# Split weights of the MLPs and the convolution in buffers of 2,112 instead of 2,048 bytes, so that they start at all multiples of 64 modulo 512

## The chip, the cores and the metric

The kernel runs on one NeuronCore of one Trainium2 chip. The metric is the device time of one execution in microseconds. Most executions of one program agree within 0.3%.

## The reference

Two layers of a trunk on x of 512 tokens by 1,024 channels, float32. Layer 0 mixes with sparse attention, layer 1 with a convolution; behind each mixer stands an MLP with squared ReLU. Cut to what matters here:

```python
h = x
for i in range(2):
    hn = rmsnorm(h, norm_mix_g[i])
    y = dsa_mixer(hn, ...) if i == 0 else conv_mixer(hn, ...)
    h = h + y
    h = h + sq_relu_mlp(rmsnorm(h, norm_mlp_g[i]), mlp_w1[i], mlp_w2[i])
return rmsnorm(h, final_g)

def sq_relu_mlp(h, w1, w2):              # w1 1024 x 4096, w2 4096 x 1024
    return jnp.square(jax.nn.relu(h @ w1)) @ w2

def conv_mixer(h, w_pw1, b_pw1, w_dw, b_dw, ln_g, ln_b, w_pw2, b_pw2):
    a = h @ w_pw1 + b_pw1                # 1024 x 2048
    u = a[..., :1024] * jax.nn.sigmoid(a[..., 1024:])
    u = causal_depthwise_conv(u, w_dw) + b_dw          # 31 taps a channel
    u = jax.nn.silu(layernorm(u, ln_g, ln_b))
    return u @ w_pw2 + b_pw2             # 1024 x 1024
```

## The kernel before

**Products in three parts.** Each float32 operand of a product is split into a high part, rounded to fp32r by ScalarE, and a low part, the difference, which VectorE (or GpSimd) makes. `split` (L80) does this for the weights: a loaded block `wraw` of 512 columns a partition becomes the tiles `whi` and `wlo`, 2,048 bytes a partition each. `mm3` (L90) then issues three fp32r matmuls, high by high (L91), high by low (L92), low by high (L93). Activations lie channel by token in tiles of 512 tokens: `hT` is the residual, `ghi`/`glo` the split normed input, `hh`/`hl` the split hidden activations of an MLP.

**Who is moving and who is stationary.** In the up-projections, in the down-projection of layer 0 and in both products of the convolution mixer the weights are stationary: 128 columns, 512 bytes a partition, a quarter of a `whi` or `wlo` tile, while 512 tokens (2,048 bytes), or 256 where the mixer works in halves, move past them. In the down-projection of layer 1 it is the other way round: 128 tokens of `hh`/`hl` are stationary and a whole `whi` or `wlo` tile of 512 columns moves; its banks are `dps`.

**Stages.** Attention of layer 0 (0 to about 275 us of the span), MLP of layer 0 (to about 640 us), convolution mixer (to about 842 us), MLP of layer 1 (to the end). An MLP is worked in four groups of 1,024 hidden channels: eight blocks up, eight blocks (layer 0) or two halves of four banks (layer 1) down, each of 8 x 3 matmuls of 512 columns a block. That makes 1,536 matmuls of 512 columns in the MLP of layer 0. In the MLP of layer 1 it is 1,488, since the first two up blocks are done in halves inside the convolution stage.

**Where the tiles lie.** A pool lays its buffers one behind the other. The pool `wsplit_att` holds five buffers each of `whi` and `wlo` for the attention; `wsplit_mid` (the second entry of the list `wsplit`) holds twelve of each from there on. `whole` rounds such tiles up to multiples of 512 bytes, and a tile `fill` of 64 bytes stands ahead of the others. In the built program all operands of fp32r matmuls start at a multiple of 512 bytes: `ghi` at 38,400 + 2,048 c, the `whi` buffers of `wsplit_mid` at 97,792 + 2,048 k, its `wlo` buffers at 122,368 + 2,048 k, with k = 0 to 11 in turn.

**The depthwise convolution.** For each of eight channel blocks c, `taps` (L753) shares 31 taps between engines. TensorE takes the first in plain float32 matmuls of 32-row diagonals `diag` by shifted copies `sh4` (L780), four of them side by side in the array. ScalarE makes products `pt` from the shifted tile `u` (L788; the first of a block goes into `pa`, L786), and GpSimd adds them into `pa` (L790). VectorE does the rest of the taps (L798 or L802), reading `u` at steps of 4 bytes. `u` tiles are 2,168 bytes long. `pt` has four buffers, so ScalarE can be four products ahead of GpSimd.

The order of instructions on an engine comes from the framework's scheduler, except where `manual_schedule` fixes it.

Of the kernel before, what the change touches and what calls it, by code (L numbers as in the profile page):

```python
# [9 lines left out]
F32 = mybir.dt.float32  # L10
F32R = mybir.dt.float32r
# [7 lines left out]
P = 128  # L19
S = 512  # L20
# [23 lines left out]
ROW = 512  # L44
FILL = 64


@with_exitstack
def kernel(
# [17 lines left out]
    def whole(n):  # L67

        return -(-4 * n // ROW) * ROW // 4
# [9 lines left out]
    wsplit = []  # L79

    def split(src, eng=None, pool=None, tag="w", bufs=None):

        a, b = src.shape[1], src.shape[2]
        hi, lo = ((pool or wsplit[-1]).tile([P, whole(a * b)], F32R, tag=tag + x, name=tag + x, bufs=bufs)
                  [:, :a * b].rearrange("p (a b) -> p a b", a=a) for x in ("hi", "lo"))
        nc.scalar.activation(hi, src, AF.Copy)  # L86
        (eng or nc.vector).tensor_sub(lo, src, hi.bitcast(F32))  # L87
        return hi, lo
# [14 lines left out]
    def proj(w, x2, eng=None, off=0):  # L103
# [7 lines left out]
        def unit(j, kh):  # L111
            i = (j + off) // 2
            j0, j1 = max(2 * i - off, 0), min(2 * i - off + 2, KC)
            if i not in raws:
                if len(raws) > 1:
                    raws.pop(next(iter(raws)))
                raws[i] = load(w, 0, KC, j0 * P, (j1 - j0) * P)
            return split(raws[i][:, kh * 4:kh * 4 + 4, (j - j0) * P:(j - j0 + 1) * P], eng)
# [46 lines left out]
    def vec(name, c=0):  # L165
        if name == "mix":
            return pm0[:, c:c + 1]
        return pv[:, vecs[name] + c:vecs[name] + c + 1]
# [51 lines left out]
    with tc.tile_pool(name="wsplit_att", bufs=5) as ws, \  # L220
# [39 lines left out]
        def v_parts(half, kb):  # L260


            ws = {}
            for k, b in kb:
                if k not in ws:
                    if k == 0:
                        vps.clear()
                    if k // 4 not in v_raw:
                        v_raw.clear()
                        v_raw[k // 4] = load(w_in, k // 4 * 4, 4, 2 * D + half * S, S)  # L270
                    ws[k] = split(v_raw[k // 4][:, k % 4:k % 4 + 1, :], nc.vector if half == 0 and k < 3 else nc.gpsimd)
                    if k == KC - 1:
                        v_raw.clear()
                if b not in vps:
                    vps[b] = bank(f"vps{b}")
                hi, lo = ws[k]
                tb = slice(b * P, (b + 1) * P)
                mm3(vps[b], ghi[k][:, tb], glo[k][:, tb], hi[:, 0, :], lo[:, 0, :], k == 0, k == KC - 1)
                yield
# [5 lines left out]
        with tc.tile_pool(name="setup", bufs=1) as setup:  # L285
# [13 lines left out]
            for i in range(4):  # L299
                xs.append(setup.tile([P, NB, 2 * P], F32, name=f"xs{i}"))  # L300
                nc.sync.dma_start(xs[i], xv[:, :, i * 2 * P:(i + 1) * 2 * P])
                t = setup.tile([P, whole(2 * nx)], F32, name=f"xw{i}")
# [4 lines left out]
            n = 0  # L307
# [20 lines left out]
            def stream(k):  # L328
                hi, lo = split(xw[k // 2][:, k % 2:k % 2 + 1, 2 * P:], nc.gpsimd, setup, "xw", 2)
                hi, lo = hi[:, 0, :], lo[:, 0, :]  # L330
                first, last = k == 0, k == KC - 1
                mm3(k_ps[:nkw], hi[:, 2 * P:], lo[:, 2 * P:], ghi[k], glo[k], first, last)
                for j in range(2):
                    js = slice(j * P, (j + 1) * P)
                    mm3(q_ps[j][:, P:], hi[:, js], lo[:, js], ghi[k][:, P:], glo[k][:, P:], first, last)
# [397 lines left out]
    with tc.tile_pool(name="cv", bufs=1) as cv, \  # L733
# [7 lines left out]
        with tc.tile_pool(name="cv_t", bufs=2) as cv_t:  # L741
# [14 lines left out]
            def taps(c, cs, npe, npool):  # L756

                u, v = us[c], vs[c][:, cs]
                n = cs.stop - cs.start
                p0 = 4 * npe  # L760
                d0 = p0 + npool

                def sh(t, more=0):
                    return u[:, cs.start + t:cs.stop + t + more]

                def wt(t):
                    return cw[:, c, t:t + 1]


                w = n + 4 * (npe - 1)  # L770
                flat = dram.tile([P, w + 3], F32, name=f"flat{c}_{cs.start}")
                nc.sync.dma_start(flat, sh(0, w + 3 - n))
                sh4 = cv_t.tile([P, 4, S + 4 * (TAPS // 4 - 1)], F32, tag="sh4", name="sh4")
                for z in range(4):
                    nc.sync.dma_start(sh4[z * 32:(z + 1) * 32, :, :w],
                                      flat.rearrange("(j i) x -> i j x", j=4)[:, :, z:z + w])
                cps = cv_ps.tile([P, S], F32, tag="conv", name="conv")[:, :n]
                for a in range(npe):
                    for j in range(4):
                        nc.tensor.matmul(cps[j * 32:(j + 1) * 32, :], diags[c][:, a, j, :], sh4[:, j, 4 * a:4 * a + n],  # L780
                                         start=a == 0, stop=a == npe - 1)
                pa = cv_t.tile([P, S], F32, tag="pa", name="pa", bufs=5)[:, :n]
                for t in range(p0, d0):
                    pt = pa if t == p0 else cv_t.tile([P, S], F32, tag="pt", name="pt", bufs=4)[:, :n]
                    if t == p0:
                        nc.scalar.activation(pt, sh(t), AF.Identity, bias=vec("bdw", c), scale=wt(t))  # L786
                    else:
                        nc.scalar.activation(pt, sh(t), AF.Copy, scale=wt(t))  # L788
                    if t > p0:
                        nc.gpsimd.tensor_add(pa, pa, pt)  # L790
                if c:
                    if npool:
                        nc.gpsimd.tensor_add(pa, pa, pilot[:, cs])
                    else:
                        nc.scalar.activation(pa, pilot[:, cs], AF.Identity, bias=vec("bdw", c))
                if c in ASIDE:
                    for t in range(d0, TAPS):
                        nc.vector.scalar_tensor_tensor(pa, sh(t), wt(t), pa, op0=OP.mult, op1=OP.add)  # L798
                    nc.vector.tensor_add(v, cps, pa)
                else:  # L800
                    for t in range(d0, TAPS - 1):
                        nc.vector.scalar_tensor_tensor(cps, sh(t), wt(t), cps, op0=OP.mult, op1=OP.add)  # L802
                    nc.vector.tensor_add(cps, cps, pa)
                    nc.vector.scalar_tensor_tensor(v, sh(TAPS - 1), wt(TAPS - 1), cps, op0=OP.mult, op1=OP.add)
# [60 lines left out]
            def first(c):  # L865
                cs = slice(0, S) if c < WHOLE else halves[0]
                taps(c, cs, *TAPS0[c])
                stat(c, cs)
# [21 lines left out]
            def second(c):  # L890
                taps(c, halves[1], *TAPS1[c])
                stat(c, halves[1])
# [146 lines left out]
```

## Time and profile before

| | |
|---|---|
| median of 3 runs | 1187.91 us (1186.22 to 1188.4) |
| the profiled execution's own time | 1186.75 us |
| its span, first to last instruction | 1185.0 us |
| mean granted TensorE clock | 0.989 |
| PE busy | 1150.8 us, 97% of the span |
| DVE busy | 663.3 us, 56% |
| ACT busy | 498.2 us, 42% |
| POOL busy | 247.5 us, 21% |

PE is TensorE's matmuls, PEld its loads of stationary operands, DVE VectorE, ACT ScalarE, POOL GpSimd. Matmuls overlap in the pipeline: one of 512 columns shows as 389 ns long, while the next starts long before. Its cost in a row of matmuls is the distance from one start to the next.

### The profile page before, as it was taken

To read this page: it belongs to the slowest core of one execution; us is meant where nothing else is said; L and a number is where in the kernel's file an instruction comes from. 1 tells how busy PE (TensorE), PEld (TensorE's weight loads), DVE (VectorE), ACT (ScalarE), POOL (GpSimd) and SP (SyncE) were. 2 spreads that over 40 slices of the span, in tenths; PEclk is the share of its full clock that TensorE was granted. 3 is DMA by queue.
4 is the path that set the end of the run, shared out by engine and by line. 5 is a ranking of instruction groups with operands and counts; after the bars stand their busy time and mean duration, and the time that the engine had idled before them with its cause. 6 is when DMAs were issued, how large, how long until landed. Compare 5 with 4: busy or idle time off the path is not lost.

```text
span 1185.0 us, 15284 instructions
## 1 busy us (share of the span) xinstructions
PE 1150.8 (97%) x5828; PEld 948.5 (80%) x5828; DVE 663.3 (56%) x1195; ACT 498.2 (42%) x936; POOL 247.5 (21%) x248
## 2 busy tenths in 40 slices
PE   7999999999999999999999988899999999999997
PEld 6778888877888888888888666689888888888886
DVE  4589854476434434434444998878544434434434
ACT  5353454545423423423435544466632432432422
POOL 2436643322005000000012667632100000000000
PEclk8999999999999999999999998999999999999999
DMA  6122222215233323322323563533322332332211
GB/s 229 36 71 72 89 84 77 71 36 182 78 100 107 98 80 107 107 83 78 125 71 116 151 172 91 161 108 115 117 86 92 107 107 72 106 107 92 86 36 71
DMA packets 104353, 117.84 MB, mean 99 GB/s; under 512 B 3817, under 2 KB 87609, under 8 KB 104280
## 3 DMA queue, kind: packets, MB, share of 16 engines
q1 hardware_dynamic: 102440, 112.89, 30.6%
q10 hardware_dynamic: 1840, 3.97, 0.9%
q8 instruction: 46, 0.75, 0.3%
q14 instruction: 27, 0.22, 0.1%
HBM read 112.56 MB, written 4.29 MB: 99 GB/s over the span
## 4 chain that ended last, share of the span: by engine, by line
PE 81%; DVE 12%; DMA 2%; issue 2%; ACT 1%; POOL 1%; SPq 0%; POOLq 0%; DVEq 0%; ACTq 0%
PE mm L91 19%; PE mm L93 19%; PE mm L92 19%; PE dps L93 5%; PE dps L92 5%; PE dps L91 5%; DVE score L482 2%; DVE m L480 2%; DVE conv L802 2%; DVE wlo L87 2%; DVE pa L798 1%; PE vps L91 1%; PE vps L92 1%; PE vps L93 1%; DMA xs<-in_x_dram 1%
## 5 line engine op out<-in xcount | busy, mean ns | idle before, releaser
L86 ACT ACTIVATE whi<-wraw 128x512 fp32r<-128x512 f32 x378 | 234.6, 631 | 469.9 <-PE mm L92 317.1
L92 PE MATMUL mm<-glo,whi 128*128 128x512 f32 (+1 forms) x928 | 337.0, 365 | 1.2 <-DVE glo L175 1.2
L93 PE MATMUL mm<-ghi,wlo 128*128 128x512 f32 (+1 forms) x928 | 337.1, 365 | 0.0
L91 PE MATMUL mm<-ghi,whi 128*128 128x512 f32 (+1 forms) x928 | 334.6, 366 | 1.9 <-ACT whi L86 0.8
L87 DVE TENSOR_TENSOR wlo<-wraw,whi 128x512 fp32r<-128x512 f32 x325 | 233.5, 726 | 177.7 <-ACT whi L86 174.1
L92 PEld LDWEIGHTS mm<-glo,whi 128*128 128x128 f32 x928 | 175.0, 189 | 31.0 <-issue 2.4
L91 PEld LDWEIGHTS mm<-ghi,whi 128*128 128x128 f32 x928 | 173.1, 189 | 32.6 <-issue 2.8
L93 PEld LDWEIGHTS mm<-ghi,wlo 128*128 128x128 f32 x928 | 175.0, 189 | 28.7 <-issue 1.1
L93 PE MATMUL mm<-hh,wlo 128*128 128x512 f32 x256 | 99.6, 389 | 0.0
L92 PE MATMUL mm<-hl,whi 128*128 128x512 f32 x256 | 99.6, 389 | 0.0
L92 PE MATMUL dps<-wlo,hh 128*128 128x512 f32 x256 | 99.6, 389 | 0.0
L91 PE MATMUL mm<-hh,whi 128*128 128x512 f32 x256 | 99.1, 389 | 0.0
L91 PE MATMUL dps<-whi,hh 128*128 128x512 f32 x256 | 99.1, 389 | 0.0
L93 PE MATMUL dps<-whi,hl 128*128 128x512 f32 x256 | 98.6, 389 | 0.0
L636 DVE SCALAR_TENSOR_TENSOR hr<-mm,rmsb 128x512 f32<-128x512 f32 x64 | 44.1, 691 | 91.9 <-PE mm L93 90.2
L87 POOL TENSOR_TENSOR wlo<-wraw,whi 128x512 fp32r<-128x512 f32 x53 | 70.9, 1342 | 89.6 <-ACT whi L86 89.5
L183 POOL TENSOR_TENSOR fr<-v,mhalf 128x1 f32<-128x1 f32 x4 | 2.2, 548 | 340.2 <-DVE v L181 340.2
L642 DVE TENSOR_TENSOR hl<-hf,hh 128x512 fp32r<-128x512 f32 x64 | 44.6, 697 | 41.9 <-ACT hh L641 41.9
L206 POOL TENSOR_TENSOR ss<-sq 128x512 f32<-128x512 f32 (+1 forms) x4 | 5.7, 1434 | 270.3 <-ACT sq L201 270.3
L790 POOL TENSOR_TENSOR pa<-pa,pt 128x512 f32<-128x512 f32 (+1 forms) x43 | 53.6, 1249 | 32.6 <-ACT pt L788 30.5
L92 PEld LDWEIGHTS mm<-hl,whi 128*128 128x128 f32 x256 | 48.0, 188 | 10.1
L92 PEld LDWEIGHTS dps<-wlo,hh 128*128 128x128 f32 x256 | 48.0, 188 | 10.0
(257 smaller groups left out, 1588.2 us busy)
## 6 DMA issues: line engine op xcount, KB each, us to landing
wraw<-in_mlp_w_dram SPq DMA_DIRECT2D x64, 1024.0 KB, 5.2
wraw<-in_conv_w_pw_dram SPq DMA_DIRECT2D x12, 1024.0 KB
wraw<-in_dsa_w_in_dram SPq DMA_DIRECT2D x10, 1024.0 KB, 9.1
wraw<-in_dsa_w_out_dram SPq DMA_DIRECT2D x4, 1024.0 KB, 4.9
sh<-flat SPq DMA_DIRECT2D x12, 260.0 KB, 3.6
sh<-flat SPq DMA_DIRECT2D x20, 138.0 KB, 2.8
xw<-in_dsa_w_in_dram ACTq DMA_DIRECT2D x4, 584.0 KB, 7.4
xs<-in_x_dram SPq DMA_DIRECT2D x4, 512.0 KB, 12.1
```

What stands on the lines that cost most here:

```text
L86: nc.scalar.activation(hi, src, AF.Copy)
L87: (eng or nc.vector).tensor_sub(lo, src, hi.bitcast(F32))
L91: nc.tensor.matmul(ps, wh, xh, start=start, stop=False)
L92: nc.tensor.matmul(ps, wh, xl, start=False, stop=False)
L93: nc.tensor.matmul(ps, wl, xh, start=False, stop=stop)
L480: nc.vector.max(m8s[-1], score[i])
L482: nc.vector.match_replace(score[i], m8s[i - 1], score[i], TAKEN)
L636: nc.vector.scalar_tensor_tensor(r, ps, 0.0, rr[0], op0=OP.max, op1=OP.mult)
L642: nc.vector.tensor_sub(tl, f, th.bitcast(F32))
L790: nc.gpsimd.tensor_add(pa, pa, pt)
L798: nc.vector.scalar_tensor_tensor(pa, sh(t), wt(t), pa, op0=OP.mult, op1=OP.add)
L802: nc.vector.scalar_tensor_tensor(cps, sh(t), wt(t), cps, op0=OP.mult, op1=OP.add)
```

## The change

Two things are done. In `split`, a tile that comes from `wsplit_mid` is 16 floats (64 bytes) longer than its contents, so its buffers step by 2,112 bytes; tiles of the attention's pool, and those that are given a pool of their own, stay as they were. To make room (12 x 2 x 64 = 1,536 bytes a partition), `pt` has three buffers of 2,048 bytes instead of four.

```diff
 ROW = 512
 FILL = 64
 
+STEP = 16
+
...
     def split(src, eng=None, pool=None, tag="w", bufs=None):
 
         a, b = src.shape[1], src.shape[2]
-        hi, lo = ((pool or wsplit[-1]).tile([P, whole(a * b)], F32R, tag=tag + x, name=tag + x, bufs=bufs)
+        hi, lo = ((pool or wsplit[-1]).tile([P, whole(a * b) + (0 if pool or len(wsplit) < 2 else STEP)], F32R, tag=tag + x, name=tag + x, bufs=bufs)
                   [:, :a * b].rearrange("p (a b) -> p a b", a=a) for x in ("hi", "lo"))
...
                 for t in range(p0, d0):
-                    pt = pa if t == p0 else cv_t.tile([P, S], F32, tag="pt", name="pt", bufs=4)[:, :n]
+                    pt = pa if t == p0 else cv_t.tile([P, S], F32, tag="pt", name="pt", bufs=3)[:, :n]
```

In the built program the `whi` buffers of `wsplit_mid` now start at 97,792 + 2,112 k and the `wlo` buffers at 123,136 + 2,112 k. Modulo 512 that is 64 k for `whi` and 256 + 64 k for `wlo`, so the two tiles of one split differ by 256. The twelve buffers of both together are 99 x 512 bytes, so what lies behind them moves by 1,536 bytes and keeps its place modulo 512. All other operands of fp32r matmuls stay at multiples of 512.

The order of instructions stays the same outside the convolution stage, on every engine. Line numbers rise by two. On ScalarE, at the start of the convolution stage, the rows before are these (`u_5532` to `u_5534` are the tiles `u` of channel blocks 0 to 2, `tg` and `pa` the gate and the partial sum):

```order
L786 ACTIVATE pa<-u_5532,pv,cw 128x512
L788 ACTIVATE pt<-u_5532,cw 128x512 x4
L86 ACTIVATE whi<-wraw 128x512 x2
L748 ACTIVATE tg<-tg,pv 128x512
L86 ACTIVATE whi<-wraw 128x512
L786 ACTIVATE pa<-u_5533,pv,cw 128x512
L788 ACTIVATE pt<-u_5533,cw 128x512 x4
L86 ACTIVATE whi<-wraw 128x512
L788 ACTIVATE pt<-u_5533,cw 128x512 x2
L86 ACTIVATE whi<-wraw 128x512 x2
```

And with the change:

```order
L788 ACTIVATE pa<-u_5532,pv,cw 128x512
L790 ACTIVATE pt<-u_5532,cw 128x512 x3
L88 ACTIVATE whi<-wraw 128x512
L790 ACTIVATE pt<-u_5532,cw 128x512
L88 ACTIVATE whi<-wraw 128x512
L750 ACTIVATE tg<-tg,pv 128x512
L88 ACTIVATE whi<-wraw 128x512
L788 ACTIVATE pa<-u_5533,pv,cw 128x512
L790 ACTIVATE pt<-u_5533,cw 128x512 x3
L88 ACTIVATE whi<-wraw 128x512
L790 ACTIVATE pt<-u_5533,cw 128x512 x3
L88 ACTIVATE whi<-wraw 128x512 x2
```

The fourth product of a block moves behind one split of weights; the number of products and splits is the same. On TensorE one place in the whole program differs, in the same stage, where a group of depthwise matmuls (`conv`) stands between the products of the first pointwise convolution. Before:

```order
L91 MATMUL mm<-ghi_106,whi 128x512
L92 MATMUL mm<-glo_114,whi 128x512
L93 MATMUL mm<-ghi_106,wlo 128x512
L780 MATMUL conv<-sh_5730,diag_2806 32x512 x8
L91 MATMUL mm<-ghi_107,whi 128x512
```

And with the change:

```order
L93 MATMUL mm<-ghi_106,whi 128x512
L94 MATMUL mm<-glo_114,whi 128x512
L782 MATMUL conv<-sh_5730,diag_2806 32x512 x8
L95 MATMUL mm<-ghi_106,wlo 128x512
L93 MATMUL mm<-ghi_107,whi 128x512
```

The eight depthwise matmuls move ahead of one product. On VectorE three splits and two steps of the gate move by a tap or two in that stage, and on GpSimd one addition changes its place.

## Rows read from the trace of the kernel before

**Rows 1.** The page: busy tenths and granted clock in 40 slices

```profile
PE   7999999999999999999999988899999999999997
...
PEclk8999999999999999999999998999999999999999
```

**Rows 2.** Chain that ended last: share of the span, by engine

```profile
PE 81%; DVE 12%; DMA 2%; issue 2%; ACT 1%; POOL 1%; SPq 0%; POOLq 0%; DVEq 0%; ACTq 0%
```

**Rows 3.** Windows: stretch, its us, each engine's busy us (instructions), clock, DMA share, GB/s

```profile
380.00:630.00 250.00, 250.00 (x1105) 207.01 (x1104) 110.95 (x165) 91.01 (x150) 8.84 (x11) 1.00 0.31 97
860.00:1170.00 310.00, 310.00 (x1369) 256.72 (x1368) 127.10 (x192) 100.84 (x168) 0.00 (x0) 1.00 0.26 85
655.00:720.00 65.00, 55.77 (x325) 39.56 (x327) 64.44 (x83) 32.55 (x53) 44.87 (x32) 0.96 0.59 157
720.00:770.00 50.00, 47.15 (x460) 33.96 (x452) 42.95 (x78) 20.30 (x40) 32.39 (x35) 0.92 0.46 125
770.00:842.00 72.00, 69.81 (x591) 67.50 (x592) 55.77 (x128) 49.21 (x106) 22.05 (x21) 1.00 0.38 125
```

**Rows 4.** Timeline of TensorE in the MLP of layer 0: start us, length us, what

```profile
372.22 0.39 PE L92 MATMUL mm<-glo,whi 128*128 128x512 f32 x1
372.44 0.39 PE L93 MATMUL mm<-ghi,wlo 128*128 128x512 f32 x1
372.67 0.39 PE L91 MATMUL mm<-ghi,whi 128*128 128x512 f32 x1
...
375.39 0.39 PE L91 MATMUL mm<-ghi,whi 128*128 128x512 f32 x1
```

**Rows 5.** Timeline of TensorE in the convolution stage, halves of 256 columns

```profile
737.28 1.94 PE L780 MATMUL conv<-sh,diag 128*32 128x256 f32 x32
...
740.09 0.28 PE L93 MATMUL mm<-ghi,wlo 128*128 128x256 f32 x1
...
743.57 0.28 PE L92 MATMUL mm<-glo,whi 128*128 128x256 f32 x1
743.78 2.80 PE L780 MATMUL conv<-sh,diag 128*32 128x256 f32 x48
```

**Rows 6.** Timeline of TensorE at the start of the MLP of layer 1

```profile
843.36 0.40 PE L92 MATMUL mm<-glo,whi 128*128 128x512 f32 x1
...
844.99 0.39 PE L93 MATMUL mm<-ghi,wlo 128*128 128x512 f32 x1
845.22 1.03 PE L957 MATMUL rt<-ident,hT 128*128 128x128 f32 x8
846.01 0.47 PE L91 MATMUL mm<-ghi,whi 128*128 128x512 f32 x1
846.32 0.39 PE L92 MATMUL mm<-glo,whi 128*128 128x512 f32 x1
...
848.40 0.39 PE L92 MATMUL mm<-glo,whi 128*128 128x512 f32 x1
```

**Rows 7.** Groups by line and shape: count, busy us, mean ns, idle before

```profile
L802 DVE SCALAR_TENSOR_TENSOR conv<-u,cw,conv 128x512 f32<-128x512 f32 x43 | 31.3, 747 | 4.2 <-PE conv L780 4.0
...
L470 DVE SCALAR_TENSOR_TENSOR score<-rl,wi,score 128x512 f32<-128x512 f32 x7 | 5.2, 749 | 1.6 <-ACT rl L469 1.2
```

**Rows 8.** Who waited for whom, 860 to 1170 us: total, times, longest

```profile
ACT whi L86 <- PE dps L93: 103.1, 48, 5.8
DVE wlo L87 <- ACT whi L86: 93.1, 63, 5.4
```

**Rows 9.** Tile pt: its instructions, and who waited for them

```profile
L788 ACT ACTIVATE pt<-u,cw x43: 494/710/727, 649.0 to 765.3; 128x512 f32<-128x512 f32 x29, 128x256 f32<-128x256 f32 x14
L790 POOL TENSOR_TENSOR pa<-pa,pt x43: 717/1294/1668, 649.8 to 766.3; 128x512 f32<-128x512 f32 x29, 128x256 f32<-128x256 f32 x14
...
POOL pa L790: 30.5, 8
ACT pt L788: 4.5, 6
```

## The prediction

> **What bounds the kernel now.** I read the page's slices first: PE is at nine tenths or more in nearly all of them, with the granted clock at 1.00, and dips to eight tenths only in four slices between 650 and 770 us and in the first and the last [rows 1]. The chain says the same: 81% of the span is TensorE, 12% VectorE [rows 2]. The windows then separate two kinds of stage [rows 3]. In both MLPs PE is busy for the whole stretch, 250.00 of 250.00 and 310.00 of 310.00 us, and the other engines have slack; VectorE, the next, is at 127.10 of 310. There, one matmul follows another without a gap, and the time is count times distance. In the convolution stage from 655 to 720 us VectorE is the bound (64.44 of 65.00), while PE has 9 us to spare; from 720 to 842 us PE is nearly full again. Since a matmul's shown length (0.39 us) is pipeline and not cost, the number that the whole prediction hangs on is the distance between starts. By the windows it is 250.00 / 1,105 = 226.2 ns and 310.00 / 1,369 = 226.4 ns [rows 3]; by the timeline, 15 starts from 372.22 to 375.39 us, 3.17 / 14 = 226.4 ns [rows 4].
>
> **What the distance is made of.** The halves of 256 columns start 3.48 us / 29 = 120.0 ns apart [rows 5]. Twice the columns cost 106.4 ns more, 0.416 ns a column, which is the 2.4 GHz level. So 226.4 - 2 x 106.4 = 13.6 ns of each matmul don't depend on the columns. This fixed part is the only thing in it that a changed start address could touch, if the streaming rate itself holds.
>
> **The change, part one: start addresses.** No instruction is added, and in the MLPs none is moved. What changes is where a matmul's weights begin. In the MLPs 1,536 + 1,488 = 3,024 matmuls of 512 columns read `whi` or `wlo`, 768 of them as the moving operand. `whi` is read twice and `wlo` once, and 2 of 12 `whi` buffers and 1 of 12 `wlo` buffers still fall on a multiple of 512, so 1 - (2 x 2/12 + 1/12) / 3 = 31/36, or 2,604 matmuls, get a new residue. A nanosecond on each is 2.6 us, 0.22% of the run.
>
> Before, every fp32r operand starts at residue 0 modulo 512, so the trace has no row of the new case. What it has:
>
> - Addresses that differ by multiples of 512 make no difference: the distances of the windows are averages over 1,105 and 1,369 matmuls with all twelve buffers and all four quarters of each, and they equal the 226.4 ns of the 15 [rows 3, 4].
> - The plain float32 matmuls of the depthwise convolution move `sh4` from starts 16 bytes apart past diagonals that lie 128 bytes apart. Their runs of 32 and 48 take 1.94 and 2.80 us; 16 more, four rounds of four side by side, cost 0.86 us, 215 ns a round of 256 columns [rows 5]. Streaming at one column in 0.833 ns is 213.3 ns, so 1.7 ns are left over although residues vary. That form streams at half the rate, so it is the nearest row and not the same case.
> - The engines that write and read the split tiles don't mind: VectorE's tap from `u`, shifted by steps of 4 bytes, takes 747 ns, the same form on aligned `score` tiles 749 ns [rows 7].
> - Splits are in no hurry. In the MLP of layer 1 ScalarE waits 103.1 us in 48 waits until matmuls have released a buffer, and VectorE 93.1 us for ScalarE [rows 8]; a few ns more on a split would vanish there.
>
> The bounds of this part are therefore set by distances that do occur. Below: the 13.6 ns shrink to the 1.7 ns of the depthwise rows, -11.9 x 2,604 = -31.0 us. Above: a second fixed part on each matmul with a new residue, 13.6 x 2,604 = +35.4 us. I take zero, because the row nearest in what it varies (starts off 512) shows no price, and because the fixed part is the same at 256 and 512 columns, which fits a cost at each change of matmul better than collisions along the stream.
>
> The Trainium skill, SBUF — State Buffer, section "Who interferes with whom", gives TensorE two read ports, one for the moving operand and one for the stationary one, and says that it waits for no one. By that rule alone the change of the MLPs' sum is zero; no run here has yet shown it off multiples of 512.
>
> **Part two: `pt` with three buffers.** A fourth product of a block must now wait until GpSimd has done the first addition; the new order puts a split into that place. Waiting for `pt` buffers exists already: 4.5 us in 6 waits [rows 9]. GpSimd isn't starved by it: an addition takes 1,294 ns in the median, a product 710 [rows 9], so three in hand are 3.9 us of cover. What queues behind a waiting product on ScalarE are splits of weights and the gate. At most one addition's time per chain, five chains from 720 us on where PE is nearly full, is 5 x 1.3 = 6.5 us; from 655 to 720 us VectorE is the bound and has taps to do meanwhile, and ScalarE is busy only 32.55 of 65 us [rows 3]. Below nothing: a split that now stands one product earlier comes 0.7 us sooner, at one or two places on the path, -1 us. I take +0.5, since splits were put ahead of the products that wait. The group of depthwise matmuls that goes ahead of one product, and the VectorE steps that move by a tap, change no sum: zero.
>
> **Sum.** 1186.75 us, the profiled execution's own time (span 1185.0 and 1.75 around it), + 0 + 0.5 = 1187.3. That execution lies 1.2 us below the median of the three runs, so for a median I say 1188.4 us.
>
> **Rivals.**
>
> *Slower: the matmuls lose their step.* The rows hold a second pace. After float32 matmuls cut in, fp32r ones start unevenly for a while: from 843.36 to 844.99 us 7 steps in 1.63 us, from 846.32 to 848.40 us 9 steps in 2.08 us, together 231.9 ns [rows 6], at granted clock 1.00 as in the windows around. Then they fall back to 226.4. If the even pace is a state that needs each matmul to begin like the last one, residues that change from one to the next, `whi` and `wlo` 256 apart in the same triple, would keep TensorE in the uneven one: 5.5 x 3,024 = +16.6 us, 1205 us. For it: the pace does depend on something besides columns and clock. Against: the uneven rows themselves have all operands at residue 0, so something else makes them. It decides from 0.9 ns a matmul on, which is 2.4 us. Its upper end is the second fixed part, 1224 us.
>
> *Faster: the fixed part was a collision.* If moving and stationary reads that both start at residue 0 get in each other's way, the 13.6 ns are its price, and spreading takes it away: down to the 1.7 ns of the depthwise rows at most, 1157 us; half of it 1173 us. For it: float32 rows with spread starts lack the fixed part. Against: their rate is half, and 13.6 ns would have to be the same for a moving operand of 1,024 and 2,048 bytes. The Trainium skill, TensorE: Matmul & The Clock Gate, section "Back-to-back issue gap", has a warm matmul of 512 columns at 512 / 2.4 + 2.5 = 215.8 ns, an estimate by that page. The trace doesn't agree, with 226.4; by the page, getting rid of the difference of 10.6 ns in 2,604 matmuls would end near 1161 us.
>
> *The convolution stage pays for `pt`.* All five waits reach PE: 1194 us. It needs ScalarE to be late for PE, and ScalarE is half idle there.
>
> **How the numbers follow.** That addresses don't matter to TensorE: 0.52, with 1188.4 us and a range of its own from 1185 to 1193 (part two's bounds). Slower by them: 0.28, between 1191 and 1224. Faster: 0.20, between 1157 and 1185. The range 1168 to 1214 leaves out half of the faster case and a third of the slower, 0.10 and 0.09. About 0.2% (2.4 us) is what a measurement of this kernel can tell from no change. The first case gives 0.37 within that, 0.10 slower (part two) and 0.05 faster; with the others, faster 0.24, same 0.38, slower 0.38.
>
> **What would show it.** Right: in the windows from 380 to 630 and from 860 to 1170 us about 1,105 and 1,369 matmuls again, 226 ns apart, and the convolution stage as long as before to 1 us; waits of ScalarE for `pt` grow from 4.5 us to some 10 without PE idling longer. Wrong: distances of 231 ns or more there, or of 220 or less. If only the down-projection of layer 1 (`dps`) changes, it is the moving operand's start that counts; if all but it, the stationary one's; if the distance follows the buffer, single residues.

## The result and the profile after

The kernel with the change takes 1199.36 us (median of 3 runs, 1198.39 to 1199.65), against 1187.91 before: a ratio of 1.0098 with a 95% interval of 1.0075 to 1.0121. It is slower by 11.5 us, inside the range that was given and on the side of the rival "the matmuls lose their step", not of the forecast of no change. The profiled execution has a span of 1197.6 us at a mean granted clock of 0.992.

The windows of the kernel after, with the columns of [rows 3]; the second one lies 10 us later, as the stage now does:

```profile
380.00:630.00 250.00, 250.00 (x1084) 203.27 (x1083) 109.40 (x164) 89.78 (x148) 9.51 (x12) 1.00 0.29 93
870.00:1180.00 310.00, 310.00 (x1343) 251.89 (x1343) 125.50 (x190) 99.66 (x166) 0.00 (x0) 1.00 0.26 85
```

TensorE is busy all the time, at the same clock, as before, and gets through fewer matmuls: 250.00 / 1,084 = 230.6 ns and 310.00 / 1,343 = 230.8 ns from start to start, where it was 226.2 and 226.4. (The windows also count matmuls that their edges cut, so they read some 0.3 ns low: a long even row of starts before has 226.7.) It waits for nobody new. What waits for it does so a little longer: ScalarE's splits wait for matmuls as they did in [rows 8], and VectorE for the splits. The first two lines of who waited for whom, 870 to 1180 us:

```profile
ACT whi L88 <- PE dps L95: 105.9, 48, 5.9
DVE wlo L89 <- ACT whi L88: 96.0, 62, 5.6
```

The stages from start to start, worked out from the two traces: the MLP of layer 0 from its first up matmul to its last down matmul, the MLP of layer 1 from its third up block to its last matmul, the convolution stage between the two:

```
                         before     after
attention, to its end    274.85    275.15 us
MLP of layer 0           360.08    366.76
convolution stage        204.01    203.20
MLP of layer 1           338.82    345.26
end of the span         1184.97   1197.58
```

The two MLPs lose 6.7 and 6.4 us, 13.1 together; spread over 3,024 matmuls that is 4.3 ns on each. The convolution stage is shorter by 0.8 us.

The timeline shows how. Two stretches of TensorE in the MLP of layer 0, after the change; in the first (up to the start at 392.62 us, which belongs to the next split) `whi` starts at 0 modulo 512 and `wlo` at 256, in the second (from 398.17 us) `whi` at 320 and `wlo` at 64, and `ghi` and `glo` at 0 in both. Modulo 256 the weights are at 0 in the first and at 64 in the second:

```profile
391.94 0.39 PE L93 MATMUL mm<-ghi,whi 128*128 128x512 f32 x1
392.17 0.39 PE L94 MATMUL mm<-glo,whi 128*128 128x512 f32 x1
392.40 0.39 PE L95 MATMUL mm<-ghi,wlo 128*128 128x512 f32 x1
392.62 0.39 PE L93 MATMUL mm<-ghi,whi 128*128 128x512 f32 x1
...
398.17 0.39 PE L93 MATMUL mm<-ghi,whi 128*128 128x512 f32 x1
398.41 0.39 PE L94 MATMUL mm<-glo,whi 128*128 128x512 f32 x1
398.64 0.39 PE L95 MATMUL mm<-ghi,wlo 128*128 128x512 f32 x1
...
400.51 0.39 PE L94 MATMUL mm<-glo,whi 128*128 128x512 f32 x1
```

At 0 three steps take 0.68 us, 226.7 ns each; at 64 ten steps take 2.34 us, 234 ns each, and evenly so. The pace follows the buffer. Grouped over both MLPs by what the stationary operand's start is above the moving one's, modulo 256, the mean distance of 512-column matmuls in the kernel after is:

```
difference         0      64     128     192
weights stand   228.7   233.0   232.8   229.4 ns
weights move    230.1   233.1   231.5   230.3 ns
```

One thing was told wrongly ahead of the prediction. The buffers aren't taken in a plain turn: in the built programs, before and after, k goes 0, 11, 10 and so on down to 5 through most of the MLP of layer 0, and the four splits behind those take `whi` from buffers 4, 1, 2, 3 and `wlo` from 1, 2, 4, 3; later the turn is another, and in some splits the two differ as well. So the two tiles of one split don't always differ by 256. In 75 of the pool's 314 splits they differ modulo 256 as well: the split at 300.90 us has `whi` at 106,240 and `wlo` at 125,248, which is 0 and 64 modulo 256. The table goes by the start of each matmul's own operands, so it isn't touched by this.

The trace also shows what happens at a switch. At 389.87 us the difference goes from 64 to 0, and the first seven distances are 236, 224, 231, 236, 228, 233 and 231 ns; only then come 226 and 227. A split is used up after 12 matmuls, so much of its time goes by before the pace has settled. That, together with the splits whose two tiles differ, is why difference 0 stands at 228.7 in the table and not at 226.7.

This made the theory for the experiments. **Difference**: the distance is set by the start of the stationary operand minus that of the moving one, modulo 256. Its rivals: **change** (the rival as it was on record: an even pace needs each matmul to start like the last), **own start** (the stationary operand's own residue), and that the missing fourth buffer of `pt` is to blame.

### The profile page after: what moved, and what is told of

It reads as the page before. It is cut to its first block, busy times and chain, and to the rows that moved or that the text cites. A ratio compares the mean times of both kernels' runs of the same rounds, so it can differ in the third digit from the quotient of the medians.

```text
span 1197.6 us, 15284 instructions
## 1 busy us (share of the span) xinstructions
PE 1161.1 (97%) x5828; PEld 946.1 (79%) x5828; DVE 664.0 (55%) x1195; ACT 498.2 (42%) x936; POOL 248.6 (21%) x248
## 5 line engine op out<-in xcount | busy, mean ns | idle before, releaser
L89 DVE TENSOR_TENSOR wlo<-wraw,whi 128x512 fp32r<-128x512 f32 x325 | 233.3, 725 | 184.8 <-ACT whi L88 181.3
L93 PEld LDWEIGHTS mm<-ghi,whi 128*128 128x128 f32 x928 | 172.6, 188 | 33.6 <-issue 1.9
L95 PEld LDWEIGHTS mm<-hh,wlo 128*128 128x128 f32 x256 | 48.1, 188 | 11.2
```

What stands on the lines that cost most here:

```text
L93: nc.tensor.matmul(ps, wh, xh, start=start, stop=False)
L95: nc.tensor.matmul(ps, wl, xh, start=False, stop=stop)
```

## The experiments

All kernels but the scans and lo64, which have one run each, were timed repeatedly against the kernel before on the same chip. Most have three buffers of `pt`, as the change has.

**pt3: the second part of the change alone.** Contents of `whi` and `wlo` as before:

```diff
-STEP = 16
+STEP = 0
```

> Three buffers of pt, all weights back at multiples of 512. If start addresses made the loss (any of the three theories on them): matmuls in the MLPs 226.4 ns apart, 1186 to 1191 us. If the convolution stage pays for pt: the distance is 226.4 ns too, but the time stays near 1199 us.

Measured: 1187.05 us, ratio 0.999 (0.9981 to 0.9998). The windows of this kernel:

```profile
380.00:630.00 250.00, 250.00 (x1104) 207.02 (x1103) 111.00 (x165) 90.95 (x149) 10.97 (x14) 1.00 0.31 97
860.00:1170.00 310.00, 310.00 (x1370) 256.68 (x1369) 128.23 (x194) 102.01 (x170) 0.00 (x0) 1.00 0.26 85
```

The counts are those of before. The loss comes from the start addresses; a buffer of `pt` fewer costs nothing that can be measured here. If anything it gains 0.1%.

**w64: all weights 64 bytes off, always.** A tile of 64 bytes ahead of `wsplit_mid` and one of 448 behind it:

```diff
-STEP = 16
+STEP = 0
...
+    ahead = ctx.enter_context(tc.tile_pool(name="ahead", bufs=1))
+    nc.gpsimd.memset(ahead.tile([P, 16], F32, name="ahead"), 0.0)
     wsplit.append(ctx.enter_context(tc.tile_pool(name="wsplit_mid", bufs=12)))
+    behind = ctx.enter_context(tc.tile_pool(name="behind", bufs=1))
+    nc.gpsimd.memset(behind.tile([P, 112], F32, name="behind"), 0.0)
```

> All whi and wlo of the MLPs and the convolution mixer start at 64 modulo 512, always the same; everything else at 0. Theory 'difference' (the start of the stationary operand minus that of the moving one, modulo 256, sets the distance; read from the changed kernel: 0 gives 226.7 ns, 64 gives 233.3, 192 gives 229): 233.3 ns in the up-projections and in the down-projection of layer 0 (2,256 matmuls, +15.3 us), 229 ns in the down-projection of layer 1, where weights move and the difference is -64 = 192 (768 matmuls, +2 us), up to 5 us more in the halves of the convolution stage: 1205 to 1211 us. Theory 'change' (the even pace is lost where residues change from one matmul to the next): none changes here, so 226.4 ns and 1188 us. Theory 'own start' (the stationary operand's own start modulo 256): 233.3 ns where weights are stationary, 226.4 ns in the down-projection of layer 1, 1203 to 1208 us.

Measured: 1204.63 us, ratio 1.0131 (1.0114 to 1.0148). Within a projection no difference changes from one matmul to the next, and yet it is the slowest of all. Its windows and a stretch of its timeline:

```profile
380.00:630.00 250.00, 250.00 (x1073) 201.40 (x1073) 108.83 (x162) 89.13 (x146) 10.41 (x15) 1.00 0.29 93
870.00:1180.00 310.00, 310.00 (x1336) 250.93 (x1335) 127.10 (x192) 100.52 (x168) 0.00 (x0) 1.00 0.26 85
```

```profile
946.18 0.40 PE L94 MATMUL mm<-glo,whi 128*128 128x512 f32 x1
...
951.78 0.40 PE L94 MATMUL mm<-glo,whi 128*128 128x512 f32 x1
```

250.00 / 1,073 = 233.0 ns in the MLP of layer 0; in an up-projection of layer 1, 24 steps in 5.60 us, 233.3 ns. "Change" doesn't make the loss. The total fell a little below what "difference" gave, since the convolution stage didn't pay: its matmuls of 256 columns came at 115.8 ns instead of 119.9, and the stage took 202.8 us. One thing doesn't fit a bare rule: in the down-projection of layer 1, where the difference is 192 throughout, the steps are 233 and 234 ns in two of the four groups and a cycle of 226, 229 and 232 in the other two. Each rhythm is held for all 192 matmuls of a group, and the mean is 231.2 where 229 was expected.

**all64: every tile of the kernel 64 bytes further.**

```diff
-FILL = 64
+FILL = 128
...
-STEP = 16
+STEP = 0
```

> The tile fill is 128 bytes instead of 64, so that every tile of the kernel, moving and stationary, starts 64 bytes later; three buffers of pt. 'Difference' and 'change': all differences are 0 and nothing changes from one to the next, 226.4 ns and 1186 to 1191 us. 'Own start': 233.3 ns everywhere in the MLPs, about 3,024 x 6.9 ns = 21 us more, 1209 us.

Measured: 1188.64 us, ratio 0.9998 (0.9988 to 1.0009). Its windows:

```profile
380.00:630.00 250.00, 250.00 (x1105) 207.07 (x1104) 111.58 (x166) 91.33 (x150) 11.58 (x16) 1.00 0.30 96
860.00:1170.00 310.00, 310.00 (x1370) 256.68 (x1369) 129.10 (x195) 102.72 (x171) 0.00 (x0) 1.00 0.26 87
```

Weights at 64 are not slow in themselves: with everything else at 64 too, the distance is 226.2 ns again. "Own start" is out; what counts is how the two operands lie to each other.

**scan16: every 16 bytes.** Buffers of 2,304 bytes, contents put 0 to 240 bytes into them; `pt` has two buffers and `pa` four, to make room:

```diff
+            n, o = whole(a * b) + 64, turn[0] // 4 % 16 * 4
+            turn[0] += 1
+        hi, lo = ((pool or wsplit[-1]).tile([P, n], F32R, tag=tag + x, name=tag + x, bufs=bufs)
+                  [:, o:o + a * b].rearrange("p (a b) -> p a b", a=a) for x in ("hi", "lo"))
```

> A reading of distances by start, not of the total (pt has two buffers and pa four, to make room): weights start at 0, 16, 32 to 240 modulo 256, each start held for two blocks (some 48 matmuls) before the next. 'Difference': a distance of its own for each start, settled within a dozen matmuls: 226.7 ns at 0, 233.3 at 64, about 232.5 at 128, 229 at 192 where weights are stationary; mirrored in the down-projection of layer 1 (229 at 64, 233.3 at 192). 'Change': 226.4 ns at every start but for the first dozen matmuls. Starts between the multiples of 64 have not been seen; if one lies below 226.4 ns, a version with it is faster than both kernels.

Measured in its one run, of 1203.58 us: mean distances in ns where the weights stand, 512 columns, from the eleventh matmul of a run with the same difference on (38 to 167 each), worked out from starts in its trace:

```
  0   227.3     64   233.2    128   233.2    192   228.9
 16   228.9     80   231.8    144   233.5    208   233.2
 32   233.3     96   234.2    160   233.2    224   233.2
 48   233.3    112   233.3    176   229.9    240   227.8
```

Where the weights move, difference 64 gives 233.3 and 192 gives 229.0, as where they stand; the weights' own start is 192 in the first and 64 in the second, so it is mirrored as "difference" has it. A broad level near 233 ns with two wells, around 0 and around 192. None lies below the 226.7 ns at which a long row with equal starts settles.

Two of the values are mixtures. At 16 one run of 48 matmuls, interrupted at its start by others, goes at 233.3 ns; the three that follow straight on a run at 0 go at 226.9. At 240 one run goes at 226.7, the others at 228.2 to 228.8. So one and the same difference can hold one pace or another.

**scan4: every 4 bytes around 0.** The same with

```diff
-            n, o = whole(a * b) + 64, turn[0] // 4 % 16 * 4
+            n, o = whole(a * b) + 64, (turn[0] // 8 % 16 - 8) % 64
```

> A reading of distances by start, not of the total: as the scan in steps of 16, but weights start at -32, -28 to +28 bytes around the multiples of 256, each held for eight splits. 'Difference' with a smooth well at 0: 226.7 ns at 0, rising to 227.8 at -16 and 228.9 at +16, between those at 4 to 12 bytes. 'Lines' (only the 16-byte line in which a read starts counts): the same 226.7 ns from 0 to +12, and 227.8 at -16 to -4. If a start lies below 226.4 ns, a version with it is faster than before.

Measured in its one run, of 1202.92 us, where the weights stand: -8 233.3, -4 227.0, 0 226.8, +4 232.2, +8 230.7, +12 231.9, +16 233.3 ns. Neither a smooth well nor lines of 16 bytes: 4 bytes to one side already cost 5 ns. The +12 is a mixture too, 233.4 in layer 0 and 229.9 in layer 1. At +16 the difference now gave 233.3 throughout, without a run at 0 just before it. Further out, -28 held 226.7 for 96 matmuls in layer 0 and ran at 230.6 in layer 1. No start lies below 0, but 0 isn't alone.

At this grain the mirror fails. Where the weights move and start 4 bytes further on, the difference is -4 as well, and the distance is 236.6 ns over 72 matmuls instead of 227.0. Where they move and start 12 bytes earlier, at difference 12, it is 239.8 instead of 229.9 to 233.4. "Difference" is borne out at multiples of 64, but for the two rhythms of w64; in finer steps it also counts which of the two operands is off.

**bufs11 and halves64: can a difference be used?** In w64 the matmuls of 256 columns had become faster. Eleven buffers of 2,304 bytes leave the choice of an offset for each split; the control has it at 0 everywhere, the other at 64 bytes for the splits that are used in halves alone:

```diff
-            return split(raws[i][:, kh * 4:kh * 4 + 4, (j - j0) * P:(j - j0 + 1) * P], eng)
+            return split(raws[i][:, kh * 4:kh * 4 + 4, (j - j0) * P:(j - j0 + 1) * P], eng, at=16 if j in half else 0)
...
-    wsplit.append(ctx.enter_context(tc.tile_pool(name="wsplit_mid", bufs=12)))
+    wsplit.append(ctx.enter_context(tc.tile_pool(name="wsplit_mid", bufs=11)))
...
-            pw2 = proj(conv_w_pw2[0], g2)
+            pw2 = proj(conv_w_pw2[0], g2, half=range(KC))
```

> Control for the next run: eleven buffers each of whi and wlo of 2,304 bytes, so that starts alternate between 0 and 256 modulo 512; three buffers of pt. 'Difference modulo 256': 226.7 ns in the MLPs, 1185 to 1190 us unless the twelfth buffer is missed. 'Change' (starts that vary from one matmul to the next cost the even pace): uneven distances near 231 ns, 1200 us.

> As the control, but splits whose matmuls have 256 columns (blocks 5 to 7 of the first pointwise product, the second one, the two up blocks of layer 1 done in halves) are put 64 bytes into their buffers; all others at 0 or 256. From the earlier runs matmuls of 256 columns took 120 ns at difference 0 and 116 at 64. 'Difference': MLPs 226.7 ns, halves 116 ns, 768 x 4 = 3 us less at most, and 1 to 3 us below the control, since the convolution stage was 1.2 us shorter with all weights at 64; 1184 to 1187 us. If the stage is bound by VectorE there: as the control.

Measured: the control 1189.24 us, ratio 1.0 (0.9991 to 1.0009). The windows of its two MLPs:

```profile
380.00:630.00 250.00, 250.00 (x1105) 207.01 (x1104) 110.11 (x165) 90.80 (x150) 8.80 (x11) 1.00 0.30 94
860.00:1170.00 310.00, 310.00 (x1369) 256.76 (x1369) 127.88 (x193) 101.35 (x169) 0.00 (x0) 1.00 0.27 85
```

That is 226.2 and 226.4 ns, although starts go to and fro between 0 and 256. It bears out the modulus of 256, and speaks against "change" once more. With the halves at 64 bytes 1188.34 us, ratio 0.9995 (0.9985 to 1.0005). Matmuls of 256 columns do come at 115.9 instead of 119.9 ns. The windows of the convolution stage, control first:

```profile
655.00:720.00 65.00, 59.99 (x354) 40.82 (x353) 63.06 (x85) 32.79 (x52) 46.93 (x34) 0.95 0.62 162
720.00:770.00 50.00, 43.05 (x445) 33.66 (x447) 42.18 (x78) 21.11 (x42) 31.07 (x34) 0.93 0.48 136
770.00:842.00 72.00, 69.57 (x583) 66.69 (x572) 54.33 (x126) 48.97 (x105) 20.65 (x20) 1.00 0.34 110
```

```profile
655.00:720.00 65.00, 57.97 (x337) 39.07 (x339) 61.62 (x82) 32.79 (x53) 46.94 (x34) 0.95 0.62 163
720.00:770.00 50.00, 42.07 (x445) 33.06 (x437) 41.81 (x77) 20.50 (x41) 30.29 (x33) 0.93 0.48 135
770.00:842.00 72.00, 68.74 (x598) 65.27 (x591) 55.78 (x128) 49.48 (x105) 21.18 (x21) 1.00 0.35 111
```

TensorE is busy 3.8 us less (172.6 against 168.8 in the three stretches), which is the 768 x 4 ns = 3.1 us of the halves and some more, but the stage isn't shorter in the profiled executions (204.2 us in the control, 204.9 here): what TensorE saves there becomes its idle time. By the medians the kernel is 0.9 us below the control, which the two intervals don't tell from nothing. No version here is more than 0.1% faster than the kernel before.

**lo64: which pair counts?** `whi` at 0, `wlo` at 64, by a tile of 64 bytes between the two in the pool:

```diff
+        if not pool and len(wsplit) > 1 and not pads:
+            pads.append(wsplit[-1].tile([P, 16], F32, tag="pad", name="pad", bufs=1))
+            nc.gpsimd.memset(pads[0], 0.0)
```

> whi always at 0 and wlo always at 64 modulo 512, three buffers of pt. Which pair counts? 'Load': the weights loaded while a matmul streams, against what that matmul moves. Then in a triple with stationary weights the second matmul (high by low, during which wlo is loaded) is the long one, 233 ns, the others 226.7. 'Own': a matmul's own weights against what it moves; the third (low by high) is long. Either way a mean near 229 ns where weights are stationary, some 1195 us. If both are uneven, the phase of the pipeline carries over and the pair can't be told from this.

Measured: 1201.65 us in one run. The window in the MLP of layer 0:

```profile
380.00:630.00 250.00, 250.00 (x1083) 203.19 (x1082) 109.40 (x163) 89.62 (x148) 9.56 (x13) 1.00 0.29 93
```

That is 250.00 / 1,083 = 230.8 ns. In the MLP of layer 0 the three matmuls of a triple are followed at 228.4, 229.2 and 235.8 ns on average, in a fixed rhythm. The third, low by high, is the long one, as "own" has it; but the other two, whose operands both start at 0, are 2 ns longer than in a pure row, and the second, during which the 64-off weights are loaded, isn't the worst. The pairs can't be taken apart further by this: part of the cost is carried on. The kernel after has the same rhythm where `whi` and `wlo` differ in this way: from 302.28 us on 228, 230, 235, 229, 229 and 236 ns.

## Why the prediction was right or wrong

**The bound and the unit were right.** The MLPs are count times distance, and nothing hides it: the windows say 250.00 / 1,084 - 250.00 / 1,105 = 4.4 ns and 310.00 / 1,343 - 310.00 / 1,369 = 4.4 ns a matmul, and 4.4 x 3,024 = 13.3 us is close to the 13.1 us that the two stages lose.

**That the time fell inside the range was luck.** The case that gave 1188.4 us had a range of its own up to 1193, and 1199.36 lies outside it. The wide range held it because it took in most of two rivals, neither of which came true as it was told. The sign for "wrong" was set too far out as well: 231 ns or more, where 230.6 and 230.8 already cost 13 us. One sign did come: the distance follows the buffer. In reading the slices, the eights are three and not four, from 681 to 770 us, and the first and the last are at seven tenths; nothing hangs on it.

**The step that failed is the zero for the start addresses.** It was chosen between -31.0 and +35.4 us, and the measured term is +13.1. Both reasons for it fell. The depthwise rows, taken as the nearest because their starts vary, stream at half the rate and foretold nothing of fp32r; that warning stood beside them and was not heeded. And the fixed part isn't the same at 256 and 512 columns once the starts differ: with weights at 64 what is left beside 106.4 ns for each 256 columns is 233.3 - 2 x 106.4 = 20.5 ns at 512 columns and 115.8 - 106.4 = 9.4 ns at 256. Put otherwise, the second 256 columns then cost 233.3 - 115.8 = 117.5 ns instead of 106.4. The premise that the streaming rate holds is what gave way.

**The rival on the slower side had the price and not the mechanism.** It gave +16.6 us from the uneven rows [rows 6]. But the even pace doesn't need each matmul to begin like the last: w64 begins them all alike and runs at 233, bufs11 varies them by 256 and runs at 226. The price was near because the level for most differences, 233 ns, lies near the mean of the uneven rows, 231.9. These rows are something else: a settling. After the transposes the trace before has 236, 224, 231, 236, 228, 233 and 230 ns from 846.78 us on, with all starts equal, and the kernel after runs through the same distances to within 1 ns when the difference goes back to 0 (at 389.87 us). So a change does cost something. It is the lesser part: at difference 0 the kernel after has 2.0 ns too much where the weights stand and 3.4 where they move (575 and 199 matmuls, some 1.8 us of the 13.1). With four differences in equal shares, (227.3 + 233.2 + 233.2 + 228.9) / 4 = 230.7 ns by the scan, near the 230.6 and 230.8 of the kernel after; that is in part chance, since its runs of 12 matmuls are mostly too short to settle. The 31/36 of matmuls with a new residue were counted modulo 512; modulo 256 it is three quarters.

**The faster rival fell.** The 13.6 ns aren't the price of equal starts: at 512 columns no start in the scans is cheaper. At 256 columns equal starts do cost more, 119.9 against 115.8 ns, so there the rival had a grain of truth. The Trainium skill, TensorE: Matmul & The Clock Gate, section "Back-to-back issue gap", gives a formula for an isolated warm matmul, by which one of 512 columns would take 215.8 ns, an estimate by that page; no start brought the distance below 226.7.

**The rule on the ports.** The distance depends on how the two operands of TensorE lie to each other: 233.0 ns in w64, 226.2 in all64, at the same clock and with the same other work. The Trainium skill, SBUF — State Buffer, section "Who interferes with whom", gives the moving and the stationary operand ports of their own, and says that TensorE waits for no one. By that rule the change would have cost nothing; the measurement decides, and as a rule of time it doesn't hold here. Whether it is the two reads that wait for each other isn't shown.

**Part two was right.** pt3 shows no cost, where +0.5 us was taken, and waits of ScalarE for `pt` grew to 9.0 us, where "some 10" was said. The two lines on who waited for the tile `pt` in the kernel after, where it was 30.5 and 4.5 us [rows 9]:

```profile
POOL pa L792: 30.0, 7
ACT pt L790: 9.0, 10
```

The convolution stage kept its length to 0.8 us, with faster halves in it and no room to use them.

**What stays open.** That the pace depends on how the two starts lie to each other is shown; what in the reading of the two operands meets at which address isn't. The cost isn't a function of the difference alone: two rhythms at difference 192 in w64, two values at 16 within one scan, 2 ns carried over in lo64, and no mirror at steps of 4 bytes. That the matmuls before choose the rhythm fits the runs at 16; no experiment was made for it.

## What to carry to other kernels

Where fp32r matmuls of 512 columns follow each other without a gap, let their moving and stationary operands start at the same residue modulo 256; 0 and 64 did equally well for both. Look at the distance between starts, not at the shown length of a matmul or its busy share: both looked as before while 1% was lost. And where a trace has no row of the new case, a form that runs at another rate is no neighbour to take zero from; both signs of the bounds deserved more weight.

## What the runs showed of the hardware

- The distance of fp32r matmuls of 512 columns, at a granted clock of 1.00, depends on how the operands' starts lie to each other modulo 256: 226.7 ns when equal, about 233 for most differences in steps of 16 bytes, 229 at 192 (scan16). In steps of 4 bytes, with weights that stand, it is 227.0 with the stationary operand 4 bytes below and 232.2 with it 4 bytes above; with weights that move, 236.6 at the first of these two differences (scan4).
- At 256 columns it is the other way round: 119.9 ns when equal (bufs11), 115.8 at a difference of 64 (w64).
- One and the same difference can run in two steady rhythms and stay in either for long: 233 and 229 ns at 192, each for 192 matmuls (w64); 233.3 and 226.9 ns at 16 (scan16).
- After an interruption, or when the difference goes back to 0, about seven matmuls run unevenly, between 224 and 236 ns, before the even 226.7 (before, after).
